# Inverse roots of norms: from feature-major vectors on ScalarE to token-major values on GpSimd

## The chip, the cores and the metric

The kernel runs on one core of a Trainium2 chip. The metric is the device time of one execution in microseconds. The engines are named as in the profile: PE (TensorE), DVE (VectorE), ACT (ScalarE), POOL (GpSimd), and SP (SyncE), whose queue issues most DMAs.

## The reference

One layer of a hybrid decoder on x of 1024 tokens x 1024 features, all in float32: a mixer whose input projection is divided between a convolution group (512 features) and an RWKV-7 group (8 heads of 64), then cross attention to 256 memory tokens, then SwiGLU. Three of its norms take part in the change:

```python
def layer_norm(x, g, b):                       # conv group, over 512 features
    mean = jnp.mean(xf, axis=-1, keepdims=True)
    var = jnp.mean(jnp.square(xf - mean), axis=-1, keepdims=True)
    y = (xf - mean) * lax.rsqrt(var + LN_EPS)
...
    kk = hd(k * k_k)                           # rwkv7_mix, over the 64 features of a head
    kk = kk * lax.rsqrt(jnp.maximum(jnp.sum(kk * kk, axis=-1, keepdims=True), 1e-24))
...
    y = rwkv7_recurrence(rh, hd(w), kh, vh, kk, hd(a))
    var = jnp.mean(jnp.square(y - mean), axis=-1, keepdims=True)
    y = (y - mean) * lax.rsqrt(var + GN_EPS)   # over the 64 features of a head
```

## The kernel before

The tokens are worked in two blocks of 512. Activations are feature-major: 128 features on the partitions, tokens along the row. Matmuls with weights are split in three (`mm3`, L193 to L195): every operand is cast on ACT to fp32r (`whi`, `ahi`) and the rest is taken by DVE (`wlo`, `alo`). `feat` writes a feature-major product (`psf`), `tokmajor` a token-major one (`pst`); both take tiles of PSUM from a pool of four (`pd`). Small products share a pool of three (`pr`, tag r), the layer norm of the convolution has one tile (`pn`).

A block of the mixer goes through: the input projection (`w_in_block`); `rwkv_prep` with two calls of `norms`, each for two of the four pairs of heads, and with `decays`, `factors` and `products` (`psg`, `psbt`) for every pair; an inverse on DVE; then `rwkv_chain`, eight chunks of 64 tokens one after the other, each with the products `psp`, `psq`, `psu`, `pss`, `psy`. After every second chunk `rwkv_out` normalizes 128 tokens of Y and stores them to `yd`. Beside it run the convolution (`conv_taps`, 30 multiply-adds on DVE for each of four tiles `acc`) and `conv_norm`, which normalizes, applies SiLU by a tanh and stores `acc` to `yd`. `mix_out` then loads `yd` as `araw`, splits it (`ahi`, `alo`) and starts the output projection (`pst`). For block 0 the chain, the memory products (`psgm`, `psvw`) and the input projection of block 1 are issued together; for block 1 the feed-forward products of block 0 are issued between the steps.

Sums over a head are products with a constant of ones in two 64x64 blocks (`blk`), so that each sum comes out already spread over the 64 partitions of its head: `head_sums` (L409) splits the squares and runs two fp32r matmuls of 512 columns (`psbk`, `psbs`). The layer norm does the same with a matrix of ones in f32 (`psln`, `psln2`). The inverse root is then taken of every element of 128x512 or 128x1024 by `rsqrt` (L236): Ln, Exp and Square on ACT and two steps of a Newton correction on DVE. The tables of ACT for Ln and for Exp and Tanh are different ones, and a table load stands ahead of each change. Norms over the 1024 features of a token are already token-major: `rstd` (L229) computes one value for each token, and GpSimd raises it to the power -0.5 (`mhalf`).

A list scheduler sets each engine's order of instructions, out of its own costs and of the program's order; tiles in a ring are handed out in program order, and `rwkv_chain` comes before `conv_norm` there.

Of the kernel before, what the change touches and what calls it, by code (L numbers as in the profile page):

```python
# [9 lines left out]
F32 = mybir.dt.float32  # L10
F32R = mybir.dt.float32r
AF = mybir.ActivationFunctionType
ALU = mybir.AluOpType
# [4 lines left out]
P = 128  # L18
# [3 lines left out]
TB = 512  # L22
NB = SEQ // TB
MEM = 256
DR = 512
HP = 4
HEADS = 8
HD = 64
# [9 lines left out]
LN_EPS = 1e-5  # L38
GN_EPS = 64e-5
# [28 lines left out]
class Trunk:  # L68
# [164 lines left out]
        nc.gpsimd.tensor_tensor(r, r, self.mhalf, op=ALU.pow)  # L233
        return r

    def rsqrt(self, y, x, t):  # L236

        nc = self.nc
        nc.scalar.activation(out=t, in_=x, func=AF.Ln)
        nc.scalar.activation(out=y, in_=t, func=AF.Exp, scale=-0.5)  # L240
        nc.scalar.activation(out=t, in_=y, func=AF.Square)
        nc.vector.scalar_tensor_tensor(out=t, in0=t, scalar=-0.5, in1=x, op0=ALU.mult, op1=ALU.mult)
        nc.vector.scalar_tensor_tensor(out=y, in0=t, scalar=1.5, in1=y, op0=ALU.add, op1=ALU.mult)

    def sumsq(self, junk, src):
        ss = self.sp.tile([P, 1], F32, tag="ss", name="ss")
# [109 lines left out]
    def conv_norm(self, b, pool, acc):  # L356
        nc = self.nc
        t0 = b * TB
        tmp = lambda name: pool.tile([P, TB], F32, tag="t", bufs=2, name=name)
        add = lambda out, x, y: nc.vector.tensor_tensor(out=out, in0=x, in1=y, op=ALU.add)  # L360
        sa, sb = tmp("lnsa"), tmp("lnsb")
        add(sa, acc[0], acc[1])
        add(sb, acc[2], acc[3])
        add(sa, sa, sb)
        ps = self.pn.tile([P, TB], F32, tag="n", name="psln")
        nc.tensor.matmul(ps, self.ones, sa, start=True, stop=True)
        for j in range(4):
            nc.vector.scalar_tensor_tensor(out=acc[j], in0=ps, scalar=-1.0 / DR, in1=acc[j],
                                           op0=ALU.mult, op1=ALU.add)
        yield 6.0  # L370
        sa = tmp("lnsq")
        nc.scalar.activation(out=sa, in_=acc[0], func=AF.Square)
        for j in range(1, 4):
            sb = tmp("lnsq")
            nc.scalar.activation(out=sb, in_=acc[j], func=AF.Square)
            add(sb, sa, sb)
            sa = sb
        ps = self.pn.tile([P, TB], F32, tag="n", name="psln2")
        nc.tensor.matmul(ps, self.ones, sa, start=True, stop=True)
        rs = pool.tile([P, TB], F32, tag="hin", bufs=2, name="lnrs")  # L380
        nc.vector.tensor_scalar(rs, ps, 1.0 / DR, LN_EPS, op0=ALU.mult, op1=ALU.add)
        ry = pool.tile([P, TB], F32, tag="hin", bufs=2, name="lnry")
        self.rsqrt(ry, rs, pool.tile([P, TB], F32, tag="t", bufs=2, name="lnt"))
        yield 6.0
        for j in range(4):
            a = acc[j]
            nc.vector.tensor_tensor(out=a, in0=a, in1=ry, op=ALU.mult)
            th = pool.tile([P, TB], F32, tag="t", bufs=2, name="lnth")
            sc, bi = self.lgh[:, j:j + 1], self.cb[:, 4 + j:5 + j]
            nc.scalar.activation(out=th, in_=a, func=AF.Tanh, scale=sc, bias=bi)  # L390
            nc.scalar.activation(out=a, in_=a, func=AF.Identity, scale=sc, bias=bi)
            nc.vector.scalar_tensor_tensor(out=a, in0=th, scalar=1.0, in1=a, op0=ALU.add, op1=ALU.mult)
            nc.sync.dma_start(out=self.yd[j * P:(j + 1) * P, t0:t0 + TB], in_=a)
            yield 2.0
# [22 lines left out]
    def rwkv_prep(self, b, pool):  # L417

        nc = self.nc
        t0, c0 = b * TB, b * NCH  # L420
        flat = lambda t: t.rearrange("p c t -> p (c t)")
# [7 lines left out]
        def load(i, name):  # L429
            t = flat2(name)  # L430
            nc.sync.dma_start(out=t, in_=self.pdr[i * P:(i + 1) * P, t0:t0 + TB])
            return t
# [10 lines left out]
        for i in range(2):  # L443
# [4 lines left out]
            x = pool.tile([P, TB], F32R, tag="st%d" % i, name="st")  # L448
# [10 lines left out]
        def norms(g):  # L459
            ks = [load(4 + 2 * g + j, "k") for j in range(2)]  # L460
            pair = lambda tag, name, dt=F32: pool.tile([P, 2, TB], dt, tag=tag, name=name)
            tt, hi, lo = pair("rt", "rt"), pair("rn", "rhi", F32R), pair("ry", "rlo", F32R)
            sums = []
            for j in range(2):
                nc.scalar.activation(out=tt[:, j, :], in_=ks[j], func=AF.Square, scale=self.col("k_k", 2 * g + j))
                sums.append(self.head_sums(hi[:, j, :], lo[:, j, :], tt[:, j, :], "psbk"))
            rn, ry = pair("rn", "rn"), pair("ry", "ry")
            for j in range(2):
                nc.vector.tensor_scalar(rn[:, j, :], sums[j], 1e-24, None, op0=ALU.max)
            r2 = lambda t: t.rearrange("p j t -> p (j t)")  # L470
            self.rsqrt(r2(ry), r2(rn), r2(tt))
            for j in range(2):
                kk[2 * g + j] = ks[j], ry[:, j, :]

# [40 lines left out]
        def products(hp, aq, bk, r, gt):  # L515
# [37 lines left out]
            nc.sync.dma_start(out=self.gnd[cl, t0:t0 + TB], in_=gt)  # L553

        norms(0)
        dec = decays(0)
        for hp in range(HP):
            fac = factors(hp, *dec)
            if hp == 1:
                yield  # L560
                norms(1)
            if hp + 1 < HP:
                dec = decays(hp + 1)
            products(hp, *fac)
# [156 lines left out]
    def rwkv_out(self, t0, pool, Y):  # L721
        nc = self.nc
        gn = lambda name: pool.tile([P, HP, GW], F32, tag="gn", bufs=4, name=name)
        flat = lambda t: t.rearrange("p h t -> p (h t)")
        bv, gt = gn("bv"), gn("gt")
        for t, src in ((bv, self.bvd), (gt, self.gnd)):
            nc.sync.dma_start(out=t, in_=src[:, t0:t0 + GW].rearrange("(h p) t -> p h t", p=P))
        sq = gn("ysq")
        nc.scalar.activation(out=sq, in_=Y, func=AF.Square)
        pair = lambda name, dt: pool.tile([P, 2, TB], dt, tag="gp", name=name)  # L730
        hl = pair("yhl", F32R)
        ps = self.head_sums(hl[:, 0, :], hl[:, 1, :], flat(sq), "psbs")
        rr = pair("yrr", F32)
        rs, ry = (rr[:, i, :] for i in range(2))
        nc.vector.tensor_scalar(rs, ps, 1.0 / HD, GN_EPS, op0=ALU.mult, op1=ALU.add)
        self.rsqrt(ry, rs, flat(sq))
        for t, op in ((ry, ALU.mult), (flat(gt), ALU.mult), (flat(bv), ALU.add)):
            nc.vector.tensor_tensor(out=flat(Y), in0=flat(Y), in1=t, op=op)
        nc.sync.dma_start(out=self.yd[DR:, t0:t0 + GW].rearrange("(h p) t -> p h t", p=P), in_=Y)

# [410 lines left out]
```

## Time and profile before

| | |
|---|---|
| time of the runs | 1616.35, 1616.92, 1618.64 us (median 1616.92) |
| profiled execution | 1611.97 us |
| its span | 1610.2 us, mean granted clock of PE 0.973 |
| PE busy | 1520.1 us (94%) |
| DVE busy | 1067.1 us (66%) |
| ACT busy | 685.0 us (43%) |
| POOL busy | 57.3 us (4%) |

Times in the rows below are microseconds from the start of the span. The profiled execution is 4.95 us shorter than the median of the runs. PE in the profile is shown as busy from the start of a matmul to its modelled end, so one that follows closely overlaps the one ahead: the distance between starts is the pace. An f32 matmul can show as two records.

### The profile page before, as it was taken

The page shows a single profiled execution, that of the slowest core. Times are in us where ns is not written, and L with a number is a line of the kernel's source. Part 1 is how long each engine was busy: PE and PEld are TensorE (multiplying, and loading weights), DVE is VectorE, ACT ScalarE, POOL GpSimd, SP SyncE. Part 2 cuts the span into 40 slices and gives each one's busy share as a digit, 9 for nine tenths or more (in the row PEclk, how much of TensorE's full clock was granted, in tenths as well). Part 3 has the DMA queues.
Part 4 walks back from the last instruction along what each step waited for, and adds up shares of the span by engine and source line. Part 5 has one row for each costly group of instructions (what it writes and reads, how often), then busy time and mean ns, then how long its engine had stood idle before and what let it go on. Part 6 is the DMA issues. An engine that isn't in the chain of part 4 may idle for free.

```text
span 1610.2 us, 22606 instructions
## 1 busy us (share of the span) xinstructions
PE 1520.1 (94%) x8688; PEld 1243.2 (77%) x8688; DVE 1067.1 (66%) x1704; ACT 685.0 (43%) x1064; POOL 57.3 (4%) x102
## 2 busy tenths in 40 slices
PE   6999699999787899799999999999999999999997
PEld 5878578888566787587788777788887888888886
DVE  6699958799679455677685997646547534444445
ACT  6554423566833334545324447433435332222222
POOL 2000000000002000000100000001002000000000
PEclk9999699999899899799999999999999999999999
DMA  6555677788646235365856454535237533333331
GB/s 217 186 167 168 199 208 254 221 284 263 207 154 203 92 98 165 104 179 174 229 177 181 130 160 140 181 120 196 82 128 244 188 95 102 92 102 94 95 89 53
DMA packets 176219, 258.41 MB, mean 160 GB/s; under 512 B 68976, under 2 KB 110064, under 8 KB 176112
## 3 DMA queue, kind: packets, MB, share of 16 engines
q1 hardware_dynamic: 175152, 256.13, 51.2%
q8 instruction: 68, 1.11, 0.3%
q10 hardware_dynamic: 960, 0.85, 0.2%
q14 instruction: 39, 0.32, 0.1%
HBM read 197.10 MB, written 59.83 MB: 160 GB/s over the span
## 4 chain that ended last, share of the span: by engine, by line
PE 80%; DVE 9%; ACT 4%; DMA 4%; issue 2%; POOL 0%; SPq 0%; DVEq 0%; ACTq 0%; POOLq 0%
PE psf L193 14%; PE psf L195 14%; PE psf L194 14%; PE pst L193 10%; PE pst L194 10%; PE pst L195 10%; DVE acc L351 3%; DVE wlo L171 1%; PE psg L523 1%; PE pstr L273 1%; ACT whi L170 1%; DVE ya L768 1%; DMA xt<-in_x_dram 1%; DMA araw<-yd 1%; PE pss L700 1%
## 5 line engine op out<-in xcount | busy, mean ns | idle before, releaser
L170 ACT CAST whi<-wraw 128x1024 fp32r<-128x1024 f32 x256 | 268.4, 1050 | 585.0 <-PE psf L194 245.7
L171 DVE TENSOR_TENSOR wlo<-wraw,whi 128x1024 fp32r<-128x1024 f32 x256 | 312.6, 1222 | 276.9 <-ACT whi L170 276.3
L193 PE MATMUL psf<-ahi,whi 128*128 128x512 f32 (+1 forms) x1200 | 457.3, 383 | 15.0 <-ACT whi L170 10.4
L195 PE MATMUL psf<-ahi,wlo 128*128 128x512 f32 (+1 forms) x1200 | 456.8, 381 | 1.2 <-DVE wlo L171 1.1
L194 PE MATMUL psf<-alo,whi 128*128 128x512 f32 (+1 forms) x1200 | 457.1, 381 | 0.0
L193 PEld LDWEIGHTS psf<-ahi,whi 128*128 128x128 f32 x1200 | 228.7, 191 | 60.8 <-ACT whi L170 13.0
L195 PEld LDWEIGHTS psf<-ahi,wlo 128*128 128x128 f32 x1200 | 228.4, 190 | 44.8 <-DVE wlo L171 2.5
L194 PEld LDWEIGHTS psf<-alo,whi 128*128 128x128 f32 x1200 | 228.6, 190 | 40.9 <-issue 0.2
L351 DVE SCALAR_TENSOR_TENSOR acc<-hin,cols,acc 128x512 f32<-128x512 f32 x240 | 170.3, 744 | 6.0 <-ACT acc L349 5.8
L194 PE MATMUL pst<-wlo,ahi 128*128 128x512 f32 x384 | 151.0, 395 | 2.3 <-DVE wlo L171 2.3
L193 PE MATMUL pst<-whi,ahi 128*128 128x512 f32 x384 | 138.6, 400 | 14.6 <-ACT ahi L170 10.3
L195 PE MATMUL pst<-whi,alo 128*128 128x512 f32 x384 | 147.4, 392 | 0.0
L194 PE MATMUL pst<-wlo,fhi 128*128 128x512 f32 x352 | 137.7, 392 | 0.0
L195 PE MATMUL pst<-whi,flo 128*128 128x512 f32 x352 | 134.3, 390 | 0.0
L193 PE MATMUL pst<-whi,fhi 128*128 128x512 f32 x352 | 133.8, 393 | 0.0
L193 PEld LDWEIGHTS pst<-whi,ahi 128*128 128x128 f32 x384 | 72.7, 191 | 30.9 <-ACT ahi L170 10.6
L194 PEld LDWEIGHTS pst<-wlo,ahi 128*128 128x128 f32 x384 | 73.3, 191 | 17.6 <-DVE wlo L171 2.7
L195 PEld LDWEIGHTS pst<-whi,alo 128*128 128x128 f32 x384 | 72.0, 189 | 14.7
L233 POOL TENSOR_TENSOR rstd<-rstd,mhalf 128x1 f32<-128x1 f32 x50 | 39.5, 798 | 1225.6 <-DVE rstd L232 1219.4
L917 DVE TENSOR_TENSOR ya<-pst,ya 128x512 f32<-128x512 f32 x80 | 54.0, 687 | 35.7 <-PE pst L195 35.5
L935 DVE SCALAR_TENSOR_TENSOR ftg<-ftg,psf 128x512 f32<-128x512 f32 x44 | 30.2, 686 | 71.3 <-PE psf L195 71.1
L194 PEld LDWEIGHTS pst<-wlo,fhi 128*128 128x128 f32 x352 | 66.1, 188 | 14.2 <-DVE wlo L171 0.4
(244 smaller groups left out, 1699.3 us busy)
## 6 DMA issues: line engine op xcount, KB each, us to landing
wraw<-in_w_gu_dram SPq DMA_DIRECT2D x88, 512.0 KB, 3.7
wraw<-in_w_in_dram SPq DMA_DIRECT2D x44, 512.0 KB, 4.2
wraw<-in_w_down_dram SPq DMA_DIRECT2D x44, 512.0 KB, 3.6
am<-amd SPq DMA_DIRECT2D x16, 512.0 KB, 5.7
wraw<-in_wkv_dram SPq DMA_DIRECT2D x16, 512.0 KB, 4.6
wraw<-in_w_out_dram SPq DMA_DIRECT2D x16, 512.0 KB, 4.1
wraw<-gd SPq DMA_DIRECT2D x16, 512.0 KB, 3.7
wraw<-vwd SPq DMA_DIRECT2D x16, 512.0 KB, 3.6
```

What stands on the lines that cost most here:

```text
L170: self.nc.scalar.copy(out=hi, in_=src)
L171: self.nc.vector.tensor_tensor(out=lo, in0=src, in1=hi.bitcast(F32), op=ALU.subtract)
L193: mm(ps, w[0], x[0], start=start, stop=False)
L194: mm(ps, w[0], x[1], start=False, stop=False)
L195: mm(ps, w[1], x[0], start=False, stop=stop)
L233: nc.gpsimd.tensor_tensor(r, r, self.mhalf, op=ALU.pow)
L273: nc.tensor.transpose(ps[:, t * P:(t + 1) * P], xt[:, k * P:(k + 1) * P], self.ident)
L351: nc.vector.scalar_tensor_tensor(out=a, in0=h[:, k:k + TB], scalar=w(k), in1=a, op0=ALU.mult, op1=ALU.add)
L523: nc.tensor.matmul(pg[g][:, i, :], bk[half[g], c + i, :], aq[half[g], :, c + i, :], start=True, stop=True)
L700: nc.tensor.matmul(ps[rows, j, :], bt[:, j, g, :], uv[:, o, :], start=True, stop=True)
L917: nc.vector.tensor_tensor(out=y, in0=ps, in1=y, op=ALU.add)
L935: nc.vector.scalar_tensor_tensor(out=tg, in0=tg, scalar=0.5, in1=pu, op0=ALU.mult, op1=ALU.mult)
```

## The change

`rsqrt` goes. `head_powers` takes each head's sum token-major: the squares of 128 tokens are the stationary operand, two columns of `blk` the moving one, and two columns of a PSUM tile `pshp` come out, one for each head. `powers` copies the n columns to a tile `pw` (a ring of four, shared by all its callers) with the scale and the epsilon, and GpSimd raises them to -0.5 in one instruction of 128xn. `spread` brings a column back to the features: the column, broadcast to 64 (or 128) equal columns, is the stationary operand, the identity the moving one, and 64x128 (or 128x128) of PSUM come out. `norms` copies the result (`psry`) to SBUF on ACT; `rwkv_out` and `conv_norm` multiply from PSUM (`psgr`, `pslnr`). The layer norm's sums become four products of one column.

```diff
@@ -233,14 +233,29 @@
         nc.gpsimd.tensor_tensor(r, r, self.mhalf, op=ALU.pow)
         return r
 
-    def rsqrt(self, y, x, t):
-
-        nc = self.nc
-        nc.scalar.activation(out=t, in_=x, func=AF.Ln)
-        nc.scalar.activation(out=y, in_=t, func=AF.Exp, scale=-0.5)
-        nc.scalar.activation(out=t, in_=y, func=AF.Square)
-        nc.vector.scalar_tensor_tensor(out=t, in0=t, scalar=-0.5, in1=x, op0=ALU.mult, op1=ALU.mult)
-        nc.vector.scalar_tensor_tensor(out=y, in0=t, scalar=1.5, in1=y, op0=ALU.add, op1=ALU.mult)
+    def powers(self, ps, n, mul, add, op0, op1):
+
+        nc = self.nc
+        r = self.sp.tile([P, 16], F32, tag="pow", bufs=4, name="pw")[:, 0:n]
+        nc.vector.tensor_scalar(r, ps, mul, add, op0=op0, op1=op1)
+        nc.gpsimd.tensor_tensor(r, r, self.mhalf.broadcast_to([P, n]), op=ALU.pow)
+        return r
+
+    def head_powers(self, srcs, mul, add, op0=ALU.mult, op1=ALU.add):
+
+        n = 2 * len(srcs)
+        ps = self.pr.tile([P, TB], F32, tag="r", name="pshp")
+        for i, x in enumerate(srcs):
+            self.nc.tensor.matmul(ps[:, 2 * i:2 * i + 2], x, self.blk.bitcast(F32)[:, 0:65:64], start=True, stop=True)
+        return self.powers(ps[:, 0:n], n, mul, add, op0, op1)
+
+    def spread(self, ps, r, n):
+
+        w = P // n
+        for i in range(4):
+            for j in range(n):
+                c = r[:, n * i + j:n * i + j + 1].broadcast_to([P, w])
+                self.nc.tensor.matmul(ps[j * w:(j + 1) * w, i * P:(i + 1) * P], c, self.ident, start=True, stop=True)
 
     def sumsq(self, junk, src):
         ss = self.sp.tile([P, 1], F32, tag="ss", name="ss")
@@ -376,15 +391,15 @@
             add(sb, sa, sb)
             sa = sb
         ps = self.pn.tile([P, TB], F32, tag="n", name="psln2")
-        nc.tensor.matmul(ps, self.ones, sa, start=True, stop=True)
-        rs = pool.tile([P, TB], F32, tag="hin", bufs=2, name="lnrs")
-        nc.vector.tensor_scalar(rs, ps, 1.0 / DR, LN_EPS, op0=ALU.mult, op1=ALU.add)
-        ry = pool.tile([P, TB], F32, tag="hin", bufs=2, name="lnry")
-        self.rsqrt(ry, rs, pool.tile([P, TB], F32, tag="t", bufs=2, name="lnt"))
+        for i in range(4):
+            nc.tensor.matmul(ps[:, i:i + 1], sa[:, i * P:(i + 1) * P], self.ones[:, 0:1], start=True, stop=True)
+        r = self.powers(ps[:, 0:4], 4, 1.0 / DR, LN_EPS, ALU.mult, ALU.add)
         yield 6.0
+        ps = self.pn.tile([P, TB], F32, tag="n", name="pslnr")
+        self.spread(ps, r, 1)
         for j in range(4):
             a = acc[j]
-            nc.vector.tensor_tensor(out=a, in0=a, in1=ry, op=ALU.mult)
+            nc.vector.tensor_tensor(out=a, in0=a, in1=ps, op=ALU.mult)
             th = pool.tile([P, TB], F32, tag="t", bufs=2, name="lnth")
             sc, bi = self.lgh[:, j:j + 1], self.cb[:, 4 + j:5 + j]
             nc.scalar.activation(out=th, in_=a, func=AF.Tanh, scale=sc, bias=bi)
@@ -459,16 +474,15 @@
         def norms(g):
             ks = [load(4 + 2 * g + j, "k") for j in range(2)]
             pair = lambda tag, name, dt=F32: pool.tile([P, 2, TB], dt, tag=tag, name=name)
-            tt, hi, lo = pair("rt", "rt"), pair("rn", "rhi", F32R), pair("ry", "rlo", F32R)
-            sums = []
+            tt, ry = pair("rt", "rt"), pair("ry", "ry")
             for j in range(2):
                 nc.scalar.activation(out=tt[:, j, :], in_=ks[j], func=AF.Square, scale=self.col("k_k", 2 * g + j))
-                sums.append(self.head_sums(hi[:, j, :], lo[:, j, :], tt[:, j, :], "psbk"))
-            rn, ry = pair("rn", "rn"), pair("ry", "ry")
+            r = self.head_powers([tt[:, j, c * P:(c + 1) * P] for j in range(2) for c in range(4)],
+                                 1e-24, 1.0, ALU.max, ALU.mult)
             for j in range(2):
-                nc.vector.tensor_scalar(rn[:, j, :], sums[j], 1e-24, None, op0=ALU.max)
-            r2 = lambda t: t.rearrange("p j t -> p (j t)")
-            self.rsqrt(r2(ry), r2(rn), r2(tt))
+                ps = self.pr.tile([P, TB], F32, tag="r", name="psry")
+                self.spread(ps, r[:, 8 * j:8 * j + 8], 2)
+                nc.scalar.copy(out=ry[:, j, :], in_=ps)
             for j in range(2):
                 kk[2 * g + j] = ks[j], ry[:, j, :]
 
@@ -727,14 +741,10 @@
             nc.sync.dma_start(out=t, in_=src[:, t0:t0 + GW].rearrange("(h p) t -> p h t", p=P))
         sq = gn("ysq")
         nc.scalar.activation(out=sq, in_=Y, func=AF.Square)
-        pair = lambda name, dt: pool.tile([P, 2, TB], dt, tag="gp", name=name)
-        hl = pair("yhl", F32R)
-        ps = self.head_sums(hl[:, 0, :], hl[:, 1, :], flat(sq), "psbs")
-        rr = pair("yrr", F32)
-        rs, ry = (rr[:, i, :] for i in range(2))
-        nc.vector.tensor_scalar(rs, ps, 1.0 / HD, GN_EPS, op0=ALU.mult, op1=ALU.add)
-        self.rsqrt(ry, rs, flat(sq))
-        for t, op in ((ry, ALU.mult), (flat(gt), ALU.mult), (flat(bv), ALU.add)):
+        r = self.head_powers([sq[:, h, :] for h in range(HP)], 1.0 / HD, GN_EPS)
+        ps = self.pr.tile([P, TB], F32, tag="r", name="psgr")
+        self.spread(ps, r, 2)
+        for t, op in ((ps, ALU.mult), (flat(gt), ALU.mult), (flat(bv), ALU.add)):
             nc.vector.tensor_tensor(out=flat(Y), in0=flat(Y), in1=t, op=op)
         nc.sync.dma_start(out=self.yd[DR:, t0:t0 + GW].rearrange("(h p) t -> p h t", p=P), in_=Y)
```

By count, PE loses 32 fp32r matmuls of 512 columns and two f32 ones, and gains 64 of two columns, 8 of one, 128 of 64x128 and 8 of 128x128. Where instructions stand on each engine also changes. The rows below are the order of the program; `x8` is a run of eight alike. Lines of the changed kernel are higher by about 15: L258 is `spread`, L249 `head_powers`, L240 the copy to `pw`, L699 to L724 the chain, L748 the products for Y, L402 and L407 those for `acc`.

First PE at the end of block 0's mixer. Before, from the last projections of block 1 (`psf`) to the start of the output projection of block 0 (`pst`):

```order
1767 L194 MATMUL psf<-alo,whi 128x512
1768 L195 MATMUL psf<-ahi,wlo 128x512
1769 L413 MATMUL psbs<-yhl,blk 128x512
1770 L414 MATMUL psbs<-yhl,blk 128x512
1771 L193 MATMUL pst<-whi,ahi 128x512
1772 L194 MATMUL pst<-wlo,ahi 128x512
```

Now:

```order
1766 L258 MATMUL psgr<-ident,pw 64x128 x8
1767 L699 MATMUL psp<-uv,am 64x64 x8
1768 L704 MATMUL psq<-qt,Sn 64x64 x8
1769 L709 MATMUL psu<-pt,TT 64x64 x8
1770 L714 MATMUL pss<-uv,bt 64x64
1771 L724 MATMUL psy<-am,uv 64x64
1772 L714 MATMUL pss<-uv,bt 64x64 x7
1773 L724 MATMUL psy<-am,uv 64x64 x7
1774 L249 MATMUL pshp<-blk,ysq 128x2 x4
1775 L258 MATMUL psgr<-ident,pw 64x128 x8
1776 L258 MATMUL pslnr<-ident,pw 128x128 x4
1777 L193 MATMUL pst<-whi,ahi 128x512
```

The last chunk of the chain (`psp` to `psy`), which stood ahead of the last 27 `psf`, now stands behind all of them, and after it the root of the last `rwkv_out` and the spread of the layer norm, all ahead of the first `pst`.

Then DVE in the same place. Before, around the products of `acc` with the inverse root of the layer norm (`lnry`):

```order
492 L738 TENSOR_TENSOR Y<-Y,bv 128x512
493 L242 SCALAR_TENSOR_TENSOR lnt<-lnt,lnrs 128x512
494 L243 SCALAR_TENSOR_TENSOR lnry<-lnt,lnry 128x512
495 L387 TENSOR_TENSOR acc<-acc,lnry 128x512 x4
496 L702 TENSOR_TENSOR Sn<-pss,Sn 128x256
497 L714 TENSOR_TENSOR Y<-psy,yq 128x4x64
498 L707 TENSOR_TENSOR Sn<-Sn,dc 128x256
499 L392 SCALAR_TENSOR_TENSOR acc<-lnth,acc 128x512
500 L171 TENSOR_TENSOR wlo<-wraw,whi 128x1024
501 L307 SCALAR_TENSOR_TENSOR evq<-psf,cols,evq 128x511
502 L310 SCALAR_TENSOR_TENSOR evq<-carry,cols,evq 128x1
503 L392 SCALAR_TENSOR_TENSOR acc<-lnth,acc 128x512
```

Now:

```order
476 L716 TENSOR_TENSOR Sn<-pss,Sn 128x256
477 L728 TENSOR_TENSOR Y<-psy,yq 128x4x64
478 L721 TENSOR_TENSOR Sn<-Sn,dc 128x256
479 L240 TENSOR_SCALAR pw<-pshp 128x8
480 L240 TENSOR_SCALAR pw<-psln_3686 128x4
481 L748 TENSOR_TENSOR Y<-Y,psgr 128x512
482 L748 TENSOR_TENSOR Y<-Y,gt 128x512
483 L748 TENSOR_TENSOR Y<-Y,bv 128x512
484 L402 TENSOR_TENSOR acc<-acc,pslnr 128x512 x4
485 L407 SCALAR_TENSOR_TENSOR acc<-lnth,acc 128x512 x4
486 L171 TENSOR_TENSOR alo<-araw,ahi 128x512 x8
```

The four products of `acc`, which stood ahead of the last chunk's sums (`Sn`, `Y`), now stand behind these, behind the copies for both roots and behind the three products for Y, and the eight splits `alo` follow directly.

Last, PE at the second `norms` of block 0. Before, around the second pair of its sums:

```order
592 L193 MATMUL psf<-ahi,whi 128x512
593 L194 MATMUL psf<-alo,whi 128x512
594 L413 MATMUL psbk<-rhi,blk 128x512
595 L414 MATMUL psbk<-rlo,blk 128x512
596 L437 MATMUL pspr<-st,lora_hi 128x512
597 L437 MATMUL pspr<-st,lora_lo 128x512
```

Now:

```order
612 L194 MATMUL psf<-alo,whi 128x512
613 L195 MATMUL psf<-ahi,wlo 128x512
614 L249 MATMUL pshp<-blk,rt 128x2 x3
615 L258 MATMUL psry<-ident,pw 64x128 x16
616 L452 MATMUL pspr<-st,lora_hi 128x512
617 L452 MATMUL pspr<-st,lora_lo 128x512
618 L452 MATMUL pspr<-st,lora_hi 128x512
```

The spread stands right behind the sums that it depends on, and ahead of the products of the decays (`pspr`); before, nothing on PE waited for the root there.

## Rows read from the trace of the kernel before

**Rows 1.** page, part 1: busy us (share of the span) and instructions of each engine

```profile
PE 1520.1 (94%) x8688; PEld 1243.2 (77%) x8688; DVE 1067.1 (66%) x1704; ACT 685.0 (43%) x1064; POOL 57.3 (4%) x102
```

**Rows 2.** stretches: us, then PE, PEld, DVE, ACT, POOL busy, clock, DMA share, GB/s

```profile
40.00:160.00 120.00, 120.00 (x573) 97.21 (x572) 99.45 (x158) 58.80 (x83) 1.76 (x6) 1.00 0.58 174
160.00:190.00 30.00, 17.21 (x68) 11.64 (x67) 29.48 (x52) 15.97 (x26) 1.74 (x4) 0.58 0.69 209
430.00:445.00 15.00, 1.31 (x3) 0.65 (x4) 10.78 (x19) 12.35 (x19) 0.00 (x0) 0.64 0.73 236
664.00:682.00 18.00, 15.90 (x52) 10.96 (x51) 11.40 (x14) 11.92 (x15) 0.94 (x1) 0.81 0.23 74
840.00:1040.00 200.00, 200.00 (x1623) 159.94 (x1622) 155.20 (x245) 98.29 (x143) 0.00 (x0) 1.00 0.50 153
```

**Rows 3.** waits of PE, 155 to 200 us: total us, times, longest

```profile
PE psg L523 <- ACT cs L488: 6.2, 1, 6.2
PE psf L193 <- DVE alo L277: 3.6, 1, 3.6
```

**Rows 4.** waits of PE, 400 to 460 us

```profile
PE pst L193 <- ACT ahi L170: 10.3, 1, 10.3
```

**Rows 5.** waits of PE, 655 to 690 us

```profile
PE psf L195 <- DVE wlo L171: 1.1, 1, 1.1
PE pspr L437 <- ACT s L478: 1.0, 1, 1.0
```

**Rows 6.** groups by line and shape: xcount, busy us, mean ns, idle before

```profile
L239 ACT ACT_TABLE_LOAD x14 | 18.0, 1283 | 15.4 <-DVE rn L469 7.6 <-DVE yrr L735 7.6
L240 ACT ACT_TABLE_LOAD x12 | 15.4, 1283 | 0.2
L543 ACT COPY bt<-psbt 128x512 f32<-128x512 f32 x16 | 9.0, 586 | 17.1 <-PE psbt L541 11.1 <-issue 5.8
L239 ACT ACTIVATE ysq<-yrr 128x512 f32<-128x512 f32 x8 | 5.1, 632 | 0.1
L242 DVE SCALAR_TENSOR_TENSOR rt<-rt,rn 128x1024 f32<-128x1024 f32 x4 | 4.9, 1215 | 2.2 <-ACT rt L241 2.2
```

**Rows 7.** GpSimd: tile `mhalf` (min/median/max ns), timeline at 511 us, group L487

```profile
L233 POOL TENSOR_TENSOR rstd<-rstd,mhalf x50: 543/548/5402, 6.3 to 1605.3; 128x1 f32<-128x1 f32 x50
...
511.08 3.27 POOL L233 TENSOR_TENSOR rstd<-rstd,mhalf 128x1 f32<-128x1 f32 x2 [7.02 <-DVE rstd L232]
...
L487 POOL COPY dc<-Dx 128x8 f32<-128x8 f32 x8 | 4.9, 608 | 110.0 <-ACT Dx L485 110.0
```

**Rows 8.** timeline of PE: start us, us, line, output, shapes, xrecords

```profile
195.63 2.05 PE L523 MATMUL psg<-aqp,bkp 64*128 64x128 f32 x24
...
228.63 0.60 PE L582 MATMUL psv<-ident,vvt 128*128 128x128 f32 x4
...
395.10 0.69 PE L685 MATMUL psp<-uv,am 128*64 128x64 f32 x16
...
415.73 1.02 PE L379 MATMUL psln<-lnsq,ones 128*128 128x512 f32 x2
...
429.34 0.39 PE L194 MATMUL psf<-alo,whi 128*128 128x512 f32 x1
429.57 0.39 PE L195 MATMUL psf<-ahi,wlo 128*128 128x512 f32 x1
```

**Rows 9.** timeline of DVE, ACT and SP, 426 to 445 us

```profile
426.08 2.50 DVE L387 TENSOR_TENSOR acc<-acc,lnry 128x512 f32<-128x512 f32 x4
...
433.75 0.80 ACT L390 ACTIVATE lnth<-acc,convb,lgh 128x512 f32<-128x512 f32 x1
...
437.44 0.68 DVE L392 SCALAR_TENSOR_TENSOR acc<-lnth,acc 128x512 f32<-128x512 f32 x1
...
438.57 4.14 SPq L747 DMA_DIRECT2D araw<-yd  x2
...
444.06 1.14 ACT L170 CAST ahi<-araw 128x512 fp32r<-128x512 f32 x2 [2.56 <-DMA araw<-yd]
```

## The prediction

> **What bounds the kernel now.** I read the page first: PE is busy in 94% of the span, so every microsecond put on PE costs one where PE has no gap, and every other engine matters only where PE waits [rows 1]. The second view, the busy time in stretches, says where that is [rows 2]. From 40 to 160 us and from 840 to 1040 us PE is busy without a gap, at a clock of 1.00. There are three holes near the change: 160 to 190 us (17.2 of 30 busy, clock 0.58, DVE 29.5 of 30), 430 to 445 us (1.3 of 15, clock 0.64), and 664 to 682 us (15.9 of 18, clock 0.81). The third view, PE's waits, names what ends each. In the first, `psg` waits 6.2 us for ACT and `psf` 3.6 us for `alo` of DVE [rows 3]. In the second, `pst` waits 10.3 us for `ahi`, the first operand of the output projection of block 0 [rows 4]. In the third, about 1 us each for the tanh of the decays and for a weight split [rows 5]. So the change is worth what it does in three holes, less what it lays on PE elsewhere.
>
> **What goes from ACT and DVE.** ACT loses 14 + 12 table loads of L239 and L240 [rows 6] and, since Ln no longer alternates with Exp and Tanh, two more of the same kind: 28 x 1.283 = 36 us. It loses Ln, Exp and Square, 30 over 512 columns at 0.63 and 12 over 1024 at up to twice that, 19 + 15 us, and 16 casts over 512, by the same price 10 us. It gains 8 copies from PSUM at 0.59 us. Net about -75 us [rows 6]. DVE loses 54 instructions over 512 columns at 0.68 [rows 9] and 8 over 1024 at 1.22 us [rows 6], -47 us, and gains 14 tiny ones of under 0.2 us each. Of that nothing reaches the time in the 320 us in which PE has no gap. In the holes:
> - 160 to 190 us. Here DVE is the bound, and the second `norms` of block 0 holds some 5 us of its work (rlo, rn, L242, L243: 4 x 0.68 + 2 x 1.22) and 6 us of ACT's before the wait of `psg`. With these gone the `alo` that release `psf` come sooner. Against it stands a new wait: `psry` is next behind `pshp` in PE's order, so PE sits out DVE's `pw` (some 2 to 3 us, as taps stand before it) and the pow. At most all 12.8 us of idle time would go; I take -6, between -10 and -2.
> - 280 to 430 us: ACT has fewer interruptions, but mostly paces weight casts fed by DMA. I take -2.
> - 664 to 682 us: the two waits (2.1 us) come from a table load and an Ln ahead of a decay's tanh, and behind them come 13 matmuls paced at 0.43 instead of 0.23 us, 2.6 us more. I take -4, between -5.5 and -1, the lower end if `psry` waits here instead.
>
> **What PE gains and loses.** The removed matmuls are cheap: 512 columns of fp32r follow each other at 0.23 us [rows 8], a pair 0.45. The new ones are many and small. `psgr` and `psry` are f32 products of 64x128 output; the nearest row is `psg`, also 64x128, whose 24 records take 2.05 us, and the order has half as many instructions as records, so a product costs two records, 0.17 us [rows 8]. The cheapest small f32 row is `psp` with 0.043 per record, which would halve it. `pshp` has two columns but a stationary operand of 128x128: between 0.043 (`psp`) and 0.15 us (`psv`, 128x128) per record; I take 0.07 [rows 8].
> One `rwkv_out`: 8 records of `pshp` 0.6, 16 of `psgr` 1.3, less 0.45 and less some 0.1 between kinds: +1.35 us (low +0.5). One `norms`: 16 records 1.1 and 32 records 2.7, less 0.9: +3 us (low +1.1). One `conv_norm`: spread 0.7 and sums 0.4, less the f32 pair of `psln`, 1.0 [rows 8]: +0.1, and I take up to +0.5, as the spread's products have 128 rows of output in place of 64.
> Outside the holes these add as they are: the first `norms` of block 0 +3, three `rwkv_out` of block 0 +4, two `norms` of block 1 +6, chain of block 1 4 x 1.35 + 0.5 = +5.9.
>
> **The pow.** No row shows one over 4, 8 or 16 columns. One column takes 0.55 us; a pair in a stretch full of DVE work shows 3.27, 1.6 each, the worst of the fifty 5.4 [rows 7]. If columns cost nothing, 16 take 0.55; if each costs a whole instruction, 8 take 4.4 and 16 take 8.8 us. I take 1.2 for 8, nearer the instruction of one column, since 128x8 of `dc` is done in 0.6 us on the same engine [rows 7]. Between `pshp` and `psgr` PE's order mostly has 24 to 34 matmuls of 512 columns, 5.5 to 7.7 us, and 18 (4.1 us) in the shortest place of block 1: with 1.2 us all of these are covered.
>
> **The end of block 0's mixer**, the largest term. Before, conv_norm's root is free of the chain: its four products `acc`x`lnry` run from 426.08 us, beside PE's last `psf` products, which end at about 429.8 [rows 8]; the last `acc` is done at 438.1, `araw` is issued at 438.57, `ahi` starts at 444.06 and `pst` at 444.73 [rows 4, 9]. That is 15 us from the last `psf` to `pst`, 12 of them from the first product to the last `acc` (ACT does other work between), 6.7 behind it. In the new order `pw` of conv_norm stands on DVE behind `pw` of the last `rwkv_out`, and `pslnr` on PE behind the last `psgr`, and both behind the last chunk of the chain, which itself now stands behind all `psf`. From the last `psf` on everything is in series: `psgr` of the third group 1.2; `psp`, `psq`, copy, `psu`, two copies, `pss` and `psy`, addition, about 4.8, to 6.0; Square 0.7 and `pshp` 0.7, to 7.5; `pw` and pow 1.5, to 9.0; `psgr` and `pslnr` 2.3, to 11.3; three products for Y 2.1, ahead of `acc` on DVE, and the first `acc` product 0.7, to 14.1; eight ACT passes at 0.72 (they overlap a little; 0.80 each [rows 9]) and the last product 0.7, to 20.5; store, load and cast as before, 6.7, to 27. All stores of `acc` stand on SP ahead of the first `araw`, behind `yd<-Y`, so none of it overlaps.
> The last `psf` ends at 429.8 + 3 (norms) - 6 (first hole) + 4 (chain) - 2 - 3 (the last chunk is now behind it) = 425.8, and `pst` starts at 452.8 in place of 444.7: **+8 us**, in which the gains and additions of block 0 are held. In block 1 the same order stands, but 60 `psf` and 48 `pst` of the feed-forward work, some 24 us, stand between `pslnr` and `pst` there, against 17 to 20 needed: nothing.
>
> **Sum** against the profiled execution: +8 (block 0), +6 - 4 (preparation of block 1), +5.9 (chain of block 1) = +16. The profiled execution took 1611.97 us, 4.95 below the median of the runs, 1616.92; I put the 16 less a little for waits that the additions take up, 15, on the median: **1632 us**. Its own range: the first hole -10 to -2, the third -5.5 to -1, PE's additions in block 1 from +5 to +12, the tail 2 us either way: 1623 to 1642.
>
> **The rivals.**
> 1. Relief wins. All 12.8 us of idle time in the first hole go and the small products cost the price of `psp`. Then the last `psf` ends at 429.8 + 1.1 - 12 + 1.5 - 3 - 3 = 414.4, `pst` at 441 (-4), preparation +2.2 - 5.5, chain +2.5: -5, 1612 us. For it speaks DVE at 29.5 of 30 us there; against it that the new wait of `psry` lies in that very stretch. It decides from a gain of some 15 us above my terms.
> 2. Nothing measurable: the first hole gives 10, the additions come to half of mine: 1617 us.
> 3. The pow over many columns is slow, at a price per column. Then 8 columns cost 4.4 us and 4 cost 2.2, one behind the other in the tail: +5; the second `norms` +7; the `norms` of block 1, whose cover is 4.1 us, 5 us for one; the chain is just covered. +17 on top of mine: 1649 us. It decides where a pow over 8 exceeds about 4 us. For it speaks the pair of 3.27 us, against it the `dc` copy.
> [...]
>
> **Chances.** Forecast 0.60, rival 1 0.16, rival 2 0.12, rival 3 0.12. A difference under 0.2%, 3.2 us, can't be told from none. Faster: rival 1 and a little of the forecast's edge, 0.18; same: 0.12; slower: 0.70. The range leaves out the lower half of rival 1 and the upper half of rival 3: 1613 to 1648.
>
> **What would show it.** Right: `pst` of block 0 starting 5 to 10 us later than at 444.7, its wait for `ahi` longer than 10.3 us, `pslnr` behind the last `psgr`; `psgr` near 0.17 us a product; PE without a gap in the chain of block 1, the chain 5 to 6 us longer. Wrong: the hole at 160 us nearly closed and all later marks shifted left by more than 10 us (rival 1); a pow over 8 columns of over 4 us, with PE waiting on GpSimd at several places (rival 3); a tail shorter than 24 us from the last `psf` to `pst`.

## The result and the profile after

The changed kernel took 1626.92 us (median of 9 runs), the kernel before 1616.89 us in the runs beside it: ratio 1.0056, 95% interval 1.0041 to 1.0072, **10 us slower**. Forecast were 1632 us and +15. The profiled execution took 1622.72 us over a span of 1620.9 us, 10.7 more than the span before; single executions of one kernel lie up to 7.4 us from their median here, so a trace's marks are good for the place of a gain or loss, and the medians for its total.

The stretches that the prediction spoke of (columns as in [rows 2]), and PE's waits in the first two holes, after:

```profile
40.00:160.00 120.00, 120.00 (x600) 97.81 (x599) 94.68 (x152) 49.48 (x72) 5.38 (x6) 1.00 0.58 175
160.00:190.00 30.00, 22.39 (x128) 17.93 (x127) 28.50 (x52) 12.75 (x23) 6.37 (x5) 0.77 0.57 175
430.00:445.00 15.00, 5.04 (x32) 4.33 (x32) 7.57 (x16) 6.28 (x9) 2.60 (x2) 0.58 0.28 96
664.00:682.00 18.00, 18.00 (x105) 13.44 (x104) 11.08 (x17) 9.13 (x14) 3.27 (x4) 1.00 0.33 99
840.00:1040.00 200.00, 200.00 (x1694) 161.28 (x1693) 136.04 (x209) 71.45 (x109) 7.97 (x5) 1.00 0.47 141
```

```profile
PE psry L258 <- POOL pw L241: 5.2, 1, 5.2
PE psg L537 <- DVE am L540: 1.3, 1, 1.3
...
PE pst L193 <- ACT ahi L170: 12.5, 1, 12.5
PE psgr L258 <- POOL pw L241: 2.0, 1, 2.0
PE pshp L249 <- ACT ysq L743: 1.5, 1, 1.5
```

The two waits of [rows 3] are gone and `psry` has one of its own; the wait of [rows 4] grew from 10.3 to 12.5 us; those of [rows 5] are gone and the third hole is closed. ACT does a quarter less in the chain of block 1 (71 against 98 us from 840 to 1040), and PE is as full there as before: in that stretch the relief buys nothing.

PE's timeline at the end of block 0's mixer, after (start us, us):

```profile
424.81 0.39 PE L195 MATMUL psf<-ahi,wlo 128*128 128x512 f32 x1
425.13 1.09 PE L258 MATMUL psgr<-ident,pw 128*64 128x128 f32 x16
426.05 0.63 PE L699 MATMUL psp<-uv,am 128*64 128x64 f32 x16
...
431.41 1.05 PE L249 MATMUL pshp<-blk,ysq 128*128 128x2 f32 x8 [1.54 <-ACT ysq L743]
434.43 1.98 PE L258 MATMUL psgr<-ident,pw 128*64 128x128 f32 x16 [1.97 <-POOL pw L241]
436.34 2.08 PE L258 MATMUL pslnr<-ident,pw 128*128 128x128 f32 x8
450.93 0.80 PE L193 MATMUL pst<-whi,ahi 128*128 128x512 f32 x1 [12.51 <-ACT ahi L170]
```

The last `psf` ends at 425.04 (forecast 425.8), `pst` starts at 450.93 (452.8): the stretch in series is 25.9 us long, forecast 27. The granted clock was 1.00 for the first group of `psgr` (1.09 us) and 0.50 from 434.4 to 438.5 us, where the last one took 1.98 and `pslnr` 2.08 us. On DVE the products of `acc` run from 438.58, behind the three for Y:

```profile
436.53 0.69 DVE L748 TENSOR_TENSOR Y<-Y,psgr 128x512 f32<-128x512 f32 x1 [3.79 <-PE psgr L258]
...
437.98 0.69 DVE L748 TENSOR_TENSOR Y<-Y,bv 128x512 f32<-128x512 f32 x1
438.58 2.47 DVE L402 TENSOR_TENSOR acc<-acc,pslnr 128x512 f32<-128x512 f32 x4
441.56 1.40 DVE L407 SCALAR_TENSOR_TENSOR acc<-lnth,acc 128x512 f32<-128x512 f32 x2 [0.50 <-ACT acc L406]
444.54 1.40 DVE L407 SCALAR_TENSOR_TENSOR acc<-lnth,acc 128x512 f32<-128x512 f32 x2 [1.58 <-ACT acc L406]
```

Where the time goes in all can be read by lining up the weight matmuls (lines 193 to 195, 6096 records in each trace): the start of the k-th of them in one trace, less that in the trace before. The kernels of the later columns are those of the experiments below.

| at (us before) | after | E1 | E4 | E5 | E11 | E7 |
|---|---|---|---|---|---|---|
| 71 | +0.9 | +0.5 | +1.0 | +1.3 | +1.1 | +0.3 |
| 135 (behind the first norms) | +4.0 | +0.5 | +4.1 | +1.3 | +1.1 | +0.3 |
| 286 (behind the first hole) | -0.6 | +0.4 | +1.1 | +1.4 | +0.4 | +0.8 |
| 408 (end of the chain) | -5.3 | +1.0 | -4.9 | +3.1 | -6.0 | +1.6 |
| 457 (behind the first `pst`) | +7.2 | -10.0 | -2.0 | -1.5 | -6.5 | -9.3 |
| 490 | +2.1 | -10.1 | -2.3 | -5.3 | -5.0 | -9.7 |
| 626 | +1.8 | -9.9 | -2.2 | -5.1 | -5.0 | -9.4 |
| 845 (behind the preparation of block 1) | +3.3 | -9.7 | -0.5 | -3.3 | -4.9 | -9.1 |
| 1048 (behind the chain of block 1) | +10.6 | -5.0 | +5.6 | +4.9 | -0.2 | -8.1 |
| 1311 | +10.7 | -4.9 | +5.6 | +4.9 | -0.1 | -8.1 |

By the medians the six are +10.0, -12.9, -0.5, +0.6, -9.6 and -14.2. The profiled execution before lies 5 to 6 us below its kernel's medians and those of the others between 4.2 below and 4.8 above theirs, so the columns show where a kernel gains or loses, and the medians how much in all. In the trace after, 1.8 of the 10.7 us are there by 626 us; 1.5 come in the preparation of block 1 and 7.3 in its chain.

### The profile page after: what moved, and what is told of

Its sections match the earlier page's. It is cut to its first block, busy times and chain, and to the rows that moved or that the text cites. A ratio compares the mean times of both kernels' runs of the same rounds, so it can differ in the third digit from the quotient of the medians.

```text
span 1620.9 us, 23259 instructions
## 1 busy us (share of the span) xinstructions
PE 1542.3 (95%) x9068; PEld 1268.9 (78%) x9068; DVE 1028.9 (63%) x1656; ACT 619.5 (38%) x986; POOL 84.0 (5%) x116
## 4 chain that ended last, share of the span: by engine, by line
PE 88%; DVE 4%; DMA 3%; ACT 2%; issue 1%; POOL 0%; SPq 0%; DVEq 0%; ACTq 0%; POOLq 0%
PE psf L195 16%; PE psf L193 15%; PE psf L194 15%; PE pst L193 10%; PE pst L194 10%; PE pst L195 10%; PE psg L537 2%; DMA gd<-evg 1%; PE pstr L288 1%; PE pspr L452 1%; DVE acc L366 1%; ACT whi L170 1%; PE pshp L249 1%; DVE ya L778 1%; DVE wlo L171 1%
## 5 line engine op out<-in xcount | busy, mean ns | idle before, releaser
L193 PE MATMUL pst<-whi,ahi 128*128 128x512 f32 x384 | 138.7, 400 | 14.2 <-ACT ahi L170 12.5
L194 PEld LDWEIGHTS pst<-wlo,fhi 128*128 128x128 f32 x352 | 66.1, 188 | 14.2 <-DVE wlo L171 0.4
L193 PEld LDWEIGHTS pst<-whi,fhi 128*128 128x128 f32 x352 | 65.9, 188 | 14.1 <-DVE ry L509 0.2
```

Source lines behind the costliest of these rows:

```text
L193: mm(ps, w[0], x[0], start=start, stop=False)
L194: mm(ps, w[0], x[1], start=False, stop=False)
```

## The experiments

All of them are compared with the kernel before, whose medians beside them were 1616.9 to 1617.9 us.

**E1 to E3, one part of the change each**: the other two functions are put back as they were (E1 `rwkv_out` alone, E2 `norms` alone, E3 `conv_norm` alone).

```diff
 E1:  conv_norm, norms:      as before
 E2:  conv_norm, rwkv_out:   as before
 E3:  rwkv_out, norms:       as before
```

E1: 

> Only rwkv_out takes its roots token-major; norms and conv_norm are as before. Theory (PE's small products where PE has no gap are the price, some 0.8 us net for each rwkv_out of the chain of block 1, and the relief of ACT hardly reaches the time): 4 to 8 us slower than before, +6 of it between the marks 830 and 1050 us, and pst of block 0 within 3 us of its old place. Rival (the end of block 0's mixer is the loss): within 2 us of before, since the layer norm's root is free of the chain again.

E2: 

> Only norms takes its roots token-major; rwkv_out and conv_norm are as before. Theory: +3 for the first norms of block 0, -5 in the hole at 160 us, +1.4 in the preparation of block 1; in this kernel's order the layer norm's sums also stand behind the last chunk, so that pst of block 0 comes late, but most of that is given back by 476 us; -2 to +3 us in all. Rival (the late pst counts in full): +5 to +9 us. Second rival (relief is what matters): 4 us faster or more.

E3: 

> Only conv_norm takes its root token-major. In its order pslnr stands ahead of the last 24 psf. Theory: within 2 us of before, pst of block 0 within 2 us of 444.7. Rival (the change of conv_norm itself makes the end late): pst 4 to 8 us later and the time 4 to 8 us longer.

Measured: E1 **1605.0 us**, ratio 0.9924 (0.9911 to 0.9936); E2 **1623.6 us**, 1.0038 (1.0024 to 1.0052); E3 1615.8 us, 0.9992 (0.9980 to 1.0005). My theory of that hour, that PE's small products are the whole price, fell in E1: with the same small products in the chain the kernel is 12.9 us faster than before, which the rival did not expect either. E2 fits the rival, a late `pst` that counts. E3 fits the theory in its time; its `pst` starts at 447.14, 2.4 us late, where at most 2 were expected. The first `pst` of E1 and of E2:

```profile
432.65 1.98 PE L267 MATMUL psgr<-ident,pw 128*64 128x128 f32 x16 [2.89 <-POOL pw L250]
434.56 0.79 PE L193 MATMUL pst<-whi,ahi 128*128 128x512 f32 x1
```

```profile
460.27 0.80 PE L193 MATMUL pst<-whi,ahi 128*128 128x512 f32 x1 [19.08 <-ACT ahi L170]
```

E1 starts the output projection 10 us earlier than before, without a wait for `ahi`, because its layer norm is ahead. Its second sums and its products of `acc`:

```profile
397.65 1.02 PE L403 MATMUL psln<-lnsq,ones 128*128 128x512 f32 x2
...
406.80 2.50 DVE L411 TENSOR_TENSOR acc<-acc,lnry 128x512 f32<-128x512 f32 x4
```

Before, they start at 415.73 [rows 8] and 426.08 us [rows 9]. In E1's order these sums stand behind 1508 weight matmuls on PE, before behind 1584; PE waits at neither place, so the place in the order sets the time: in the trace before, the 76 between take 16.9 of the 18.1 us. The gain came by the order, which the scheduler sets anew for every kernel. Whether the shorter work of ACT moved it, or something else in the change, was not separated. E2, with neither that nor the chain in time, is 15.5 us late.

**E4, the ring.** The changed kernel, with a ring of its own for the layer norm's `pw`:

```diff
-        r = self.sp.tile([P, 16], F32, tag="pow", bufs=4, name="pw")[:, 0:n]
+        r = self.sp.tile([P, 16], F32, tag=ring, bufs=4, name="pw")[:, 0:n]
...
-        r = self.powers(ps[:, 0:4], 4, 1.0 / DR, LN_EPS, ALU.mult, ALU.add)
+        r = self.powers(ps[:, 0:4], 4, 1.0 / DR, LN_EPS, ALU.mult, ALU.add, "powc")
```

> The changed kernel with a ring of its own for the layer norm's pw tile; in the order pslnr then stands ahead of the last chunk's psu, and the products of acc ahead of its sums on DVE. Theory (of the 6.2 us by which pst came later, 4.1 were given back by 476 us at two waits that were there before): pst of block 0 about 7 us earlier than in the changed kernel, the time 1 to 3 us shorter than that of the changed kernel, so 7 to 9 over before. Rival (the late pst counts in full): 6 to 8 us shorter, 2 to 4 over before.

Measured 1617.4 us, 0.9996 (0.9985 to 1.0008), 9.5 us less than the changed kernel and more than either expectation; `pst` starts at 442.87, 8.1 us earlier, waiting 3.88 us for `ahi` in place of 12.5. So the shared ring is what puts it off, and by the medians the late `pst` counts in full. My theory had taken from the trace after that 5 us were given back between 457 and 490 us, as two waits of PE in the trace before are not in the trace after:

```profile
466.04 0.50 PE L194 MATMUL pst<-wlo,ahi 128*128 128x512 f32 x1 [2.32 <-DVE wlo L171]
...
473.07 0.50 PE L193 MATMUL pst<-whi,ahi 128*128 128x512 f32 x1 [2.21 <-DVE ss L805]
```

In E4 the second wait is there again (2.20 us) with 0.45 us of the first, and E4's lead over the changed kernel, 9.2 us at 457 us, is 4.4 at 490 and 5.1 at the end: the traces bear the theory out. The profiled execution of the changed kernel lies 4.2 us below its median, so how much is given back in most executions stays open: the ring costs 5 us by the traces and 9.5 by the medians.

**E5 and E6, the start of the chain.** Before, the first `psp` of the chain starts at 296.56, after at 307.63, though PE is ahead in its weight matmuls there. E5 is the changed kernel with the norms of block 0 as before. E6 is E1 with DVE work ahead of the inverse:

```diff
 E5: +        norms = norms_old if b == 0 else norms_new
 E6: +        if b == 0:
     +            for i in range(8):
     +                nc.vector.tensor_scalar(At, At, 1.0, None, op0=ALU.mult)
              for t in range(31):
```

E5: 

> The changed kernel with the norms of block 0 as before (block 1, rwkv_out and conv_norm stay changed, with the shared ring of pw). Theory (the norms of block 0 put off the inverse on DVE, which ends 9.6 us later, and with it the chain, whose last chunk so comes behind all psf): first psp of the chain back near 297 us, pst of block 0 near 435 to 438 us instead of 450.9, then +1.5 in the preparation of block 1 and +6.5 in its chain: 1607 to 1613 us. Rival (the shared ring ties conv_norm to the last rwkv_out in any case): 1622 to 1628 us.

E6: 

> The kernel with only rwkv_out changed, and eight products of 128x1024 by 1.0 on DVE (6 us in series) ahead of the inverse of block 0. Theory (the chain's start decides when the mixer of block 0 ends): first psp 5 to 8 us later, pst of block 0 3 to 8 us later than in that kernel, the time 3 to 8 us longer, 1608 to 1613 us. Rival (the chain has slack there, and the shared ring or the price on PE is what counts): within 1.5 us of 1605.

Measured: E5 1618.0 us, 1.0000 (0.9988 to 1.0012); E6 1615.7 us, 0.9993 (0.9978 to 1.0007). First `psp` and end of the mixer, E5:

```profile
298.23 0.69 PE L726 MATMUL psp<-uv,am 128*64 128x64 f32 x16
...
425.87 1.09 PE L267 MATMUL psgr<-ident,pw 128*64 128x128 f32 x16
426.89 1.16 PE L267 MATMUL pslnr<-ident,pw 128*128 128x128 f32 x8
443.20 0.80 PE L193 MATMUL pst<-whi,ahi 128*128 128x512 f32 x1 [11.04 <-ACT ahi L170]
```

and E6:

```profile
312.61 0.69 PE L712 MATMUL psp<-uv,am 128*64 128x64 f32 x16
...
446.36 0.80 PE L193 MATMUL pst<-whi,ahi 128*128 128x512 f32 x1
```

E5 misses both: the chain is back in time and 9 us are won, but `pslnr` still stands behind the last `psgr`, as in the changed kernel, and `pst` still waits 11 us for `ahi`. Chain and ring are two ties, and each costs when the other is undone. E6 puts the chain off by 15.6 us, more than I meant, and `pst` by 11.8; E1's 1605.0 becomes 1615.7. That the start of the chain decides is shown; how much of it is slack (some 4 us here) is rough.

**E9 to E11, both ties, and which norms.** E9 is E5 with the ring of E4. E10 and E11 are E1 with one of block 0's two calls of `norms` token-major:

```diff
 E10: +        norms = lambda g: (norms_new if b == 0 and g == 0 else norms_old)(g)
 E11: +        norms = lambda g: (norms_new if b == 0 and g == 1 else norms_old)(g)
```

E9: 

> The changed kernel with the norms of block 0 as before and with a ring of its own for the layer norm's pw; pslnr then stands 120 rows ahead of the first pst. Theory (two ties, the late chain and the shared ring, each of which leaves the end of block 0 late by itself): both undone it comes to that of the kernel with rwkv_out alone, plus 1.5 in the preparation of block 1 and 0.5 for conv_norm: 1604 to 1609 us, pst of block 0 at 433 to 437. Rival (something else in conv_norm costs the rest): 1612 us or more.

E10: 

> The kernel with only rwkv_out changed, and the first norms of block 0 token-major as well. Theory (the second call, where psry waits in a stretch in which DVE has no gap, puts off the inverse): first psp within 3 us of 297, +3 before 105 us, 1604 to 1609 us. Rival (the first call does): first psp after 303, 1612 us or more.

E11: 

> The kernel with only rwkv_out changed, and the second norms of block 0 token-major as well. Theory: the hole at 160 us is 4 to 6 us shorter, yet the first psp comes after 303 us and pst of block 0 5 to 12 us later than at 434.6: 1610 to 1617 us. Rival: first psp within 3 us of 297 and, with the shorter hole, 1600 to 1604 us.

Measured: E9 1611.5 us, 0.9970 (0.9959 to 0.9981); E10 1603.7 us, 0.9922 (0.9903 to 0.9941); E11 1607.4 us, 0.9943 (0.9924 to 0.9962). First `psp` and first `pst` of E10, then of E11:

```profile
294.30 0.69 PE L726 MATMUL psp<-uv,am 128*64 128x64 f32 x16
...
433.76 0.39 PE L193 MATMUL pst<-whi,ahi 128*128 128x512 f32 x1
```

```profile
306.59 0.69 PE L726 MATMUL psp<-uv,am 128*64 128x64 f32 x16
...
438.54 0.80 PE L193 MATMUL pst<-whi,ahi 128*128 128x512 f32 x1
```

It is the second call that puts off the chain, by 9.6 us; the first doesn't. Its price in E11 is only 2.4 us over E1 (expected 5 to 12): `rwkv_out` alone changed and a layer norm that is free leave 4 us of delay at `pst`. In the changed kernel the ring is there too, and the same lateness costs 9. E9 brings `pst` back to 435.48, as expected, and is 15.4 us faster than the changed kernel, but 6.5 slower than E1, where 2 were expected; against E5 its ring is worth 6.4 us. Its marks part from E1's by 2.5 us at 457 and 5.0 at 490, where the two kernels do the same work, by 5.1 at 626 and by 6.3 at 845, 1.2 of it for the preparation of block 1. From the first `pst` to 490 us PE waits 8.2 us in six places in E9 and 4.4 us in two in E1; why stays open.

The way by which the second call delays the chain is read from the orders and the traces, and was not varied by itself. `psry` stands ahead of the decays of the second pair and waits 5.2 us on PE; the last `psg` of the block then comes behind 693 weight matmuls in PE's order, where it stood behind 658, and since PE has no gap from 190 to 227 us, 35 more at 0.23 us are 8 us. In E11 it comes behind 688, at 224.41 us, in E10 behind 651, at 218.21. The trace before and after:

```profile
216.80 1.16 PE L523 MATMUL psg<-aqp,bkp 64*128 64x128 f32 x16
```

```profile
168.13 3.68 PE L258 MATMUL psry<-ident,pw 128*64 128x128 f32 x32 [5.21 <-POOL pw L241]
...
226.21 0.27 PE L537 MATMUL psg<-aqp,bkp 64*128 64x128 f32 x1
```

The inverse on DVE starts from these products; it ends at 285.2 in place of 275.5 us.

**E7, E8 and E12, the price on PE.** E7 is E1 with `rwkv_out` of block 1 as before. E8 is E1 with half as many products in `spread`, out of a copy of the eight columns to 128x512. E12 is E7 with a token-major `conv_norm` on a ring of its own.

```diff
 E7: +        (self.rwkv_out_new if t0 < TB else self.rwkv_out_old)(t0, pool, Y)
 E8: +    def spread(self, ps, r, n, w=None):
     +        if w is not None:
     +            self.nc.vector.tensor_copy(out=w.rearrange("p (n w) -> p n w", w=64), in_=r.unsqueeze(2).broadcast_to([P, 8, 64]))
     +        for i in range(4):
     +            c = r[:, i:i + 1].broadcast_to([P, P]) if w is None else w[:, i * P:(i + 1) * P]
     +            self.nc.tensor.matmul(ps[:, i * P:(i + 1) * P], c, self.ident, start=True, stop=True)
```

E7: 

> Only rwkv_out changed, and that in block 0 alone; in block 1 it is as before. Theory (where PE has no gap, four rwkv_out cost 4 to 5 us net and the relief of ACT and DVE gives nothing): 3 to 5.5 us shorter than with both blocks, 1599.5 to 1602 us. Rival (ACT's relief in block 1 pays for the products): within 1 us of 1605 or longer.

E8: 

> Only rwkv_out changed, in both blocks, and its spread done by four products with 128 stationary columns in place of eight with 64, out of a copy of the eight columns to 128x512 that DVE makes (0.7 us). Theory (the spread's price goes by the count of products): PE saves some 0.4 us per rwkv_out, of which the four in block 1 count: 1 to 2.5 us shorter than with eight, 1602.5 to 1604. Rival (a product of 128 rows costs as much as two of 64): within 1 us of 1605, or longer by the copy where the root is on the path.

E12: 

> Norms as before, rwkv_out token-major in block 0 alone, conv_norm token-major in both blocks with a ring of its own: what the runs so far leave as the best. Theory (the layer norm's root is covered in either form): within 2 us of 1603, 1601 to 1605. Rival (the table loads and the two DVE steps that it saves shorten the end of block 0's mixer): 1598 to 1601.

Measured: E7 **1603.2 us**, 0.9913 (0.9898 to 0.9929); E8 1610.1 us, 0.9958 (0.9944 to 0.9972); E12 1605.6 us, 0.9932 (0.9913 to 0.9950). By the marks four `rwkv_out` cost 4.7 us in the chain of block 1 in E1 (from -9.7 at 845 to -5.0 at 1048) and E7 is spared all but 1.0 of that; by the medians E7 is 1.8 better, under the 3 expected, and its interval overlaps E1's. E8 fell: a group takes as long with four products as with eight,

```profile
347.65 1.06 PE L267 MATMUL psgr<-ident,wd 128*128 128x128 f32 x8
```

against 1.09 in the trace after, and the last root comes later by the copy (`pst` at 436.73 us, in E1 at 434.56). So the eight are not dear by their count. E12, 0.6 us over its theory's range, is no better than E7: with a ring of its own a token-major layer norm gains nothing, as far as these runs can tell. E7 and E10 are the best that was run, about 14 and 13 us below the kernel before.

## Why the prediction was right

**The range, the sign and the likeliest case held**; +10 were measured, +15 forecast. By its steps:

- *The end of block 0's mixer*: +8 forecast, +6.2 at `pst` in the trace. The order, the 27 us in series (25.9) and the end of `psf` (425.8; 425.0) came as written, and E4 shows that undoing the ring takes `pst` 8.1 us back and 9.5 us off the median. Right in place and cause. The steps hold within 0.4 us up to the last `acc` (20.9 us behind the last `psf`, forecast 20.5), one of them by luck: 2.3 us stood there for `psgr` and `pslnr` together, but the products for Y waited for `psgr` alone, which took 1.98 us at a granted clock of 0.50. From the last `acc` to `pst` it took 5.0 us in place of 6.7. What the prediction didn't ask is why the last chunk had moved behind all `psf`; E10 and E11 answer that: the second `norms` (no `psf` stands behind the last chunk in E11, 48 in E10).
- *The first hole*: -6, measured -4.6 (from +4.0 to -0.6). The new wait of `psry` was there, 5.2 us, longer than taken. It was priced only by what it costs PE on the spot; that it pushes the products behind it, and with them the inverse and the chain, was missing, though the tail held the effect.
- *The first norms*: +3, measured +3.1.
- *Preparation of block 1*: +2 net, measured +1.5, the third hole closed.
- *The chain of block 1*: +5.9, measured +7.3. Two sizes behind it were off and nearly cancelled: a group of `psgr` takes 1.09 us where 1.3 was taken, and one of `pshp` 1.05 where 0.6 was.
- *The pow*: 8 columns were taken at 1.2 us and took 1.78 on the mean, 16 took 3.1, 4 took 1.0 us, in the groups of the trace after:

```profile
L241 POOL TENSOR_TENSOR pw<-pw,mhalf 128x8 f32<-128x8 f32 x8 | 14.2, 1778 | 408.4 <-DVE pw L240 408.4
L241 POOL TENSOR_TENSOR pw<-pw,mhalf 128x16 f32<-128x16 f32 x4 | 12.5, 3133 | 146.9 <-DVE pw L240 146.9
...
L241 POOL TENSOR_TENSOR pw<-pw,mhalf 128x4 f32<-128x4 f32 x2 | 2.0, 1007 | 0.0
```

At the least, 8 took 1.63 and 16 took 2.90 us. So a column more took about 0.16 us, far from a whole instruction (0.55 us for one column [rows 7]), and the cover held but for the tail, the `psry` of the second `norms` and 0.4 us at 356 us. Rival 3 is out.

- *The sum* of 16 was 5 us above the 10.7 of the traces, by the size of its largest term: the tail was counted as +8, and of the +6.2 at `pst` only 2.1 are left at 490 us. The chain of block 1, 1.4 us above its term, works the other way. So most of what is left at the end of this trace was laid on PE in block 1, and not lost in the tail.

The pow of 16 columns took 3.81 us at 164 us, among the taps, where DVE was busy throughout, and 2.91 and 2.90 at 668 and 713 us, where DVE was busy for 0.13 and 0.69 us of it. Of 8 columns, one took 2.21 us at 354 us, with DVE busy throughout, and one 1.75 at 388 us, with DVE busy for 1.69. What made the two longer was not varied.

Rival 1, that relief wins, was right about a part that I had priced at 2 us: E1, with `rwkv_out` alone on token-major values, is 10 us ahead at 457 us, as its layer norm comes earlier in the order and `ahi` is ready before PE comes to `pst`. The change as a whole loses that to the chain and the ring.

## What to carry to other kernels

When an order shows a step that has moved behind others, trace the move back to the first instruction that is late: the cause can lie 200 us ahead, in another function, and can then be undone alone. A ring of tiles shared by callers that were independent ties the later one in program order to the earlier; give each its own. Relief of an engine bought nothing in the chain of block 1, where PE has no gap (ACT was busy for 71 us in place of 98, and the chain took 7.3 us more); what was won came where PE had waited 10.3 us for `ahi`, by another order. As each call site moves the order, a change of this kind is best taken one site at a time: here one of three, `rwkv_out`, carried the whole gain.

## What the runs showed of the hardware

- An f32 product with 64 stationary columns and 128 moving ones cost half of one with 128 and 128: eight (16 records) took 1.09 us in the trace after, at a clock of 1.00, and four (8 records) 1.06 in E8. Fewer and wider products won nothing in E8 (1610.1 us, E1 1605.0).
- With 128 stationary columns it cost as much for two moving columns as for 128: 8 records of `pshp` took 1.05 us, 8 of E8's `psgr` 1.06. A product of 512 moving columns was dearer: in the trace before, the next matmul starts 0.46 us behind `psln` (at 961.39 us), and 0.23 us behind a product of `pshp` in the trace after (at 911.8 us, four in 0.914 us).
- GpSimd's power of 128xn took about 0.4 us and 0.16 us for each column, worked out from 0.54, 1.0, 1.63 and 2.90 us for 1, 4, 8 and 16 at the least; the longest were 2.21 for 8 and 3.81 for 16.
